# Last two output projections as one Strassen product inside the down projection, attention normalised by GpSimd, first two projections in groups of four

## The chip, the core and the metric

The kernel runs on one core of a Trainium2 chip, in one launch. The metric is device time in microseconds (us), the median of several runs. TensorE (PE in the profile) does the matrix products. VectorE (DVE) and ScalarE (ACT) do elementwise work and empty PSUM. GpSimd (POOL) takes some elementwise work. SyncE (SP) issues most of the DMA transfers, and POOL and ACT issue some. Each engine takes its own instructions strictly in their order and waits, with all that stands behind, for whatever its next instruction needs.

## The reference

One layer of a hybrid decoder, 2048 tokens of width 1024, all float32:

```python
    hn = rms_norm(h, mix_pre_g)
    proj = hn @ w_in
    q, k, v, u = ...
    attn_out = sliding_window_attention(q, k, v, attn_sinks, rel_bias)
    conv_out = conformer_conv(u, conv_dw, conv_dw_b, conv_ln_g, conv_ln_b, w_conv_pw)
    mixed = jnp.concatenate([attn_out, conv_out], axis=-1) @ w_out
    h = h + rms_norm(mixed, mix_post_g)
    hn = rms_norm(h, ffn_pre_g)
    ff = (jax.nn.silu(hn @ w_gate) * (hn @ w_up)) @ w_down
    h = h + rms_norm(ff, ffn_post_g)
```

Attention is banded (window 128, 8 query heads, 2 key heads, a learned sink per head); its softmax ends with `p = p / denom`. The convolution is depthwise with 31 taps on 512 channels, followed by LayerNorm, swish and a 512 x 512 product. `D_FF` is 2816.

## The kernel before

Four tiles of 512 tokens go through stages whose names carry the tile's number: A (in-projection), B (attention, in blocks of 128 tokens), T (the 31 convolution taps, `SCALAR_TENSOR_TENSOR` on DVE), C (the convolution's tail), W (output projection) with N (the two norms and the residual behind it), then for pairs of tiles H (the feed-forward's transposed operands), F (gate and up projections) and G (down projection). F0 and G0 serve tiles 0 and 1, F2 and G2 tiles 2 and 3. Stage J multiplies `w_conv_pw` into the lower half of `w_out` once (`w_join`), so that W's operand is the attention output above and the convolution's output below, kept transposed in DRAM as `mixT`.

Every float32 product is three TensorE passes: an operand is split into a high part (a copy by ACT) and a low part (a subtraction by DVE, sometimes POOL), and ah·wh, ah·wl and al·wh are accumulated in PSUM. A pass is a matmul of 128 x 128 by 128 x 512. F and G use one level of Strassen: seven products instead of eight, on sums of operand blocks.

W (`stage_w`) takes a tile's eight 128-row chunks of `mixT` two at a time (G=2): for each pair of chunks and each half of the output's columns it makes, for four blocks of 128 tokens, a PSUM group of six matmuls, and adds each group into an SBUF accumulator (the first by an ACT copy, the three others by DVE). W0 runs beside the end of A and W1 between A and F0; W2 and W3 stand in a lane beside G0, in the PSUM banks named `tr`, with accumulators in the SBUF buffers named `mid`.

N (`norm_w`) squares the accumulators on ACT, makes a reciprocal square root by some twelve tiny operations on POOL and DVE, scales on DVE, loads x and adds it, stores h, squares again, makes a second reciprocal root, scales on ACT (L841) and stores the result as `hn_scr` (L844). H (`stage_h_plain`) loads it back by columns (names `fc@H`, `at@H`), turns it on TensorE and makes the operands. Of F2 the products need B11 (from tile 2, four buffers `ql`) first and B21 (four buffers `mid`) second. `mid` is also where W3's accumulators are, so B21 of F2 can be made once tile 3's normalised rows have been stored.

F (`stage_p1`) writes each unit's products and their Strassen sums to DRAM (`mids<-fa@F`, the sums by DVE in F0 and by POOL in F2), and G (`stage_p2`) loads them back: the first two steps' operands through buffers `at`, the others through four buffers `fa`, the same that F's last sums use. G is 77 steps (7 products by 11 pairs of chunks), each 12 matmuls.

What sets the order: the main line of stages is a Python generator, and at each of its yields `run` pumps the lanes (`lb` attention, `lc` taps, `lw` projections, `lh` operands, `lt` sums, `ld` and `lf`), each at its own rate, so that the lanes' instructions are written between the main line's. A lane's stage may wait until another has come some way (`since`), and `until` writes a lane's rest at once. What is written first has priority, and a planner that works with its own durations then puts each engine's instructions in the order in which they are queued. `lc.rates` sets how early the taps of each tile are written: T3's are written slowly (RP 0.1) until F0 is over and at RC3 after.

The lines that the change touches: L518 (`vd`, the difference of neighbouring blocks of v) and L522 (the product by the reciprocal denominator, `p@B<-p@B,sm@B`) in `stage_b`; all of `stage_w`; the plan's last part, which adds W2, C3, W3 and B11.2 to `lw`, runs G0 and calls `lw.until("N3")`. Matmuls are L109 and most DVE operations L86, whoever calls them.

Of the kernel before, what the change touches and what calls it, by code (L numbers as in the profile page):

```python
# [25 lines left out]
P = 128  # L26
# [12 lines left out]
def layer_kernel(ctx, tc, x, xT, cols, rows, sinks, relb, onehot, w_in, w_pw, w_out, w_gate, w_up, w_down, out):  # L39
# [19 lines left out]
    def f4(tag, shape=(P, D)):  # L59
        return t_(tag, shape)  # L60
# [4 lines left out]
    def hl(tag):  # L65
        return t_(tag, (P, 2, T), F32R)
# [387 lines left out]
    def stage_b(t):  # L454
# [56 lines left out]
        def back(b):  # L511
# [3 lines left out]
            if not first:  # L515
                lab[0] = L
                vd = t_("vd", (P, P))
                vtt(vd, vtok[:, b], vtok[:, b + 1], ALU.subtract)  # L518
            for g in range(2):
                lab[0] = L  # L520
                hs = slice(4 * g, 4 * g + 4)
                vtt(pr[:, hs], pr[:, hs], rd[:, hs].unsqueeze(2).to_broadcast([P, 4, P]), ALU.mult)  # L522
                pg = f4("p", (P, 2, T))
                o = tr()
                for i in range(4):
                    nc.tensor.transpose(o[:, i * P : (i + 1) * P], pr[:, 4 * g + i], ident)
# [12 lines left out]
                yield 0.9  # L539
# [216 lines left out]
    def stage_w(w, spill, G, atag, htag, mtag, bank_of, norm=None):  # L756
        L = f"W{w}"
        lab[0] = L
        acc = [f4(atag) for _ in range(4)]

        def acts(gi, ms=None):
            aa = []
            for m in ms or load(gi):
                a = hl(htag)
                act(a[:, 0], m, AF.Copy)  # L765
                vtt(a[:, 1], m, a[:, 0].bitcast(F32), ALU.subtract)
                aa.append([a])
            return aa

        stage = spare_tile() if w == 1 else None  # L770

        def load(gi):
            ms = []
            for c in range(G * gi, G * gi + G):
                ms.append(stage[:, c % 2] if w == 1 else f2(mtag))
                nc.sync.dma_start(ms[-1], mixT[c, :, w * T : (w + 1) * T])
            return ms

        first = load(0)
        gb = load_gb(0) if w > 1 else None  # L780
        if w != 1:
            yield 5.0 if w == 0 else 8.0
            lab[0] = L
        nxt = acts(0, first)
        for gi in range(KC // G):
            aa = nxt
            for n in range(2):
                lab[0] = L
                if n == 0 and gi + 1 < KC // G:
                    if w < 2 and G * gi + G == 4:  # L790
                        ld.until(f"C{w}")
                        lab[0] = L
                    rows_next = load(gi + 1)
                if n == 1 and gi + 1 < KC // G:
                    nxt = acts(gi + 1, rows_next)
                src = w_out[2 * gi : 2 * gi + 2] if gi < 2 else w_join[2 * gi - 4 : 2 * gi - 2]
                ws = weight(src[:, :, n * T : (n + 1) * T].rearrange("c p t -> p c t"),
                            lo_out[n, 2 * gi : 2 * gi + 2], w > 0, on_pool=False)
                yield from block_half(acc, list(zip(aa, ws)), n, gi == 0, L, bank_of)
        tail = norm_w(w, spill, acc, mtag, gb)  # L800
        if norm:
            norm(tail)
        else:
            yield from tail

    def norm_w(w, spill, acc, mtag, gb):
# [377 lines left out]
    def stage_p2(ws, am, td, last=False):  # L1184
# [112 lines left out]
        for i in range(nn):  # L1297
            ty, pr = steps[i]
            load(i + 3)
# [91 lines left out]
    RC0, RC1, RC2, RC3, RW0, RW, RB, LC = 0.7, 1.1, 0.4, 0.9, 1.7, 1.25, 0.8, 100  # L1391
# [8 lines left out]
    RP = 0.1  # L1400
# [8 lines left out]
    JL, JS = 10, 2  # L1409
    lb = Lane(RB, 0)  # L1410
# [9 lines left out]
    lw.rates = {"W0": RW0, "C2": RW, "W2": RW, "C3": RW, "W3": RW}  # L1420
# [13 lines left out]
    lw.add("W0", stage_w(0, True, 2, "x", "hl", "fa", mm), lambda: "A3" in started and "J" in ld.done)  # L1434
# [53 lines left out]
    run(stage_w(1, True, 2, "mid", "hl", "at", mm, norm=lambda g: lh.add("N1", g)))  # L1488
# [8 lines left out]
    ws, ops = (2, 3), {}  # L1497
    lw.add("C2", stage_tail(2))
# [75 lines left out]
```

## Time and profile before

| | us |
|---|---|
| Median of three runs | 1947.46 |
| The three runs | 1943.13, 1947.46, 7967.86 |
| Profiled execution, its own time | 1948.75 |
| Profiled execution, span from first to last instruction | 1947.0 |
| PE busy | 1903.4 (98%) |
| DVE busy | 1488.2 (76%) |
| ACT busy | 971.4 (50%) |
| POOL busy | 231.7 (12%) |

The mean granted TensorE clock is 0.991. In the trace A and B fill the span up to about 440 us, W0 and W1 the time to about 550 us, F0 runs to 982 us, G0 to 1303 us, F2 to 1733 us, and G2 to the end. Each of these stages follows the one before on TensorE with no more than a few microseconds between. One of the three runs took four times as long as the others and says nothing of the kernel.

### The profile page before, as it was taken

How to read it: one execution, taken by the hardware profiler on the slowest of the kernel's cores; microseconds unless marked ns; L12 is line 12 of the kernel's file. 1: busy time of each engine (PE TensorE's matmuls, PEld its weight loads, DVE VectorE, ACT ScalarE, POOL GpSimd, SP SyncE). 2: the span in 40 equal slices, each digit the busy share in tenths (PEclk: the TensorE clock that was granted, in tenths of full speed). 3: DMA queues.
4: the chain of work that ended last, by engine and by line, in shares of the span. 5: the costliest groups of instructions: out<-in, count | busy, mean ns of one | idle time of the engine just before them, and what ended most of it. 6: DMA issues, size and time to landing. Idle time of an engine off the chain costs nothing.

```text
span 1947.0 us, 26776 instructions
## 1 busy us (share of the span) xinstructions
PE 1903.4 (98%) x8730; PEld 1538.9 (79%) x8730; DVE 1488.2 (76%) x2747; ACT 971.4 (50%) x1910; POOL 231.7 (12%) x327
## 2 busy tenths in 40 slices
PE   8999999999999999999999999999999999999997
PEld 7877776777778888878878878878888888888886
DVE  5999989897885999988569985778666665455557
ACT  5355444557667533433364556576533443345443
POOL 5100001221010000000000110010032332211000
PEclk9999999999899999999999999999999999999999
DMA  8896756579768776877487688689644443375664
GB/s 304 276 318 227 238 172 189 190 228 329 236 221 280 236 255 216 277 261 252 138 306 241 209 302 261 208 309 360 215 160 160 162 157 102 131 248 189 207 194 152
DMA packets 229181, 443.56 MB, mean 228 GB/s; under 512 B 22920, under 2 KB 48688, under 8 KB 229040
## 3 DMA queue, kind: packets, MB, share of 16 engines
q1 hardware_dynamic: 207408, 406.19, 63.1%
q10 hardware_dynamic: 19392, 28.32, 4.0%
q0 software_dynamic: 2240, 7.34, 1.0%
q8 instruction: 68, 1.11, 0.2%
q14 instruction: 73, 0.60, 0.1%
HBM read 320.64 MB, written 121.12 MB: 227 GB/s over the span
## 4 chain that ended last, share of the span: by engine, by line
PE 73%; DVE 12%; DMA 8%; issue 3%; ACT 2%; POOL 2%; SPq 0%; DVEq 0%; ACTq 0%; POOLq 0%
PE mm@F L109 36%; PE mm@G L109 16%; PE mm@A L109 8%; DVE fc@C L86 4%; PE tr@W L109 4%; PE mm@W L109 4%; PE tr@B L109 2%; DMA raw@A<-w_in 1%; PE ct@J L109 1%; DVE w@F L86 1%; DMA mixT<-fc@C 1%; DVE mid@W L86 1%; DMA at@W<-mixT 1%; DVE fa@F L86 1%; DMA hT<-gb@H 1%
## 5 line engine op out<-in xcount | busy, mean ns | idle before, releaser
L86 DVE SCALAR_TENSOR_TENSOR fc@C<-glu@C,colt,fc@C 128x512 f32<-128x512 f32 x480 | 354.7, 754 | 2.2
L109 PE MATMUL mm@F<-hl@H,w@F 128*128 128x512 f32 x1056 | 254.6, 390 | 0.8 <-ACT gb@F L1109 0.8
L109 PE MATMUL mm@G<-hl@G,hl@G 128*128 128x512 f32 x924 | 226.1, 395 | 6.1 <-DVE hl@G L86 2.2
L109 PEld LDWEIGHTS mm@F<-hl@H,w@F 128*128 128x128 f32 x1056 | 197.8, 188 | 42.3 <-ACT gb@F L1109 1.3
L109 PEld LDWEIGHTS mm@G<-hl@G,hl@G 128*128 128x128 f32 x924 | 172.3, 189 | 45.3 <-DVE hl@G L86 4.1
L109 PE MATMUL mm@A<-hl@A,w@A 128*128 128x512 f32 x840 | 204.4, 396 | 3.1 <-ACT hl@A L342 1.4
L856 ACT ACTIVATE w@F<-chl@F 128x512 fp32r<-128x512 f32 x220 | 135.5, 625 | 137.0 <-PE mm@F L109 131.6
L109 PE MATMUL mm@G<-w@G,hl@G 128*128 128x512 f32 x876 | 199.5, 389 | 0.0
L109 PEld LDWEIGHTS mm@G<-w@G,hl@G 128*128 128x128 f32 x876 | 164.4, 188 | 34.1
L109 PEld LDWEIGHTS mm@A<-hl@A,w@A 128*128 128x128 f32 x840 | 157.1, 189 | 41.3 <-issue 2.5
L86 DVE TENSOR_TENSOR w@F<-chl@F,w@F 128x512 fp32r<-128x512 f32 x198 | 144.9, 735 | 37.1 <-ACT w@F L856 36.7
L109 PE MATMUL mm@F<-ql@H,w@F 128*128 128x512 f32 x528 | 131.0, 391 | 2.5 <-ACT w@F L856 2.2
L109 PE MATMUL mm@F<-mid@H,w@F 128*128 128x512 f32 x528 | 131.0, 390 | 1.2 <-DVE mid@H L86 1.2
L109 PE MATMUL mm@F<-p@H,w@F 128*128 128x512 f32 x528 | 130.6, 393 | 0.0
L109 PE MATMUL mm@F<-x@H,w@F 128*128 128x512 f32 x528 | 128.4, 391 | 0.0
L109 PEld LDWEIGHTS mm@F<-ql@H,w@F 128*128 128x128 f32 x528 | 98.4, 188 | 23.7 <-ACT w@F L856 2.7
L109 PEld LDWEIGHTS mm@F<-p@H,w@F 128*128 128x128 f32 x528 | 100.2, 190 | 21.2 <-ACT at@F L1112 0.2
L109 PEld LDWEIGHTS mm@F<-mid@H,w@F 128*128 128x128 f32 x528 | 98.8, 188 | 22.5 <-DVE mid@H L86 1.6
L109 PEld LDWEIGHTS mm@F<-x@H,w@F 128*128 128x128 f32 x528 | 98.6, 188 | 21.9 <-issue 0.8
L156 ACT ACTIVATE w@A<-raw@A 128x512 fp32r<-128x512 f32 x110 | 67.5, 626 | 85.8 <-PE mm@A L109 51.4
L86 DVE TENSOR_TENSOR w@G<-raw@G,w@G 128x512 fp32r<-128x512 f32 x73 | 51.0, 699 | 68.3 <-ACT w@G L856 67.4
L109 PE MATMUL mm@W<-w@W,hl@W 128*128 128x512 f32 x384 | 99.5, 406 | 2.3 <-ACT hl@W L765 2.3
(307 smaller groups left out, 3188.4 us busy)
## 6 DMA issues: line engine op xcount, KB each, us to landing
mids<-fa@F SPq DMA_DIRECT2D x154, 256.0 KB, 2.6
raw@A<-w_in SPq DMA_DIRECT2D x55, 512.0 KB, 4.8
w@A<-lo_in SPq DMA_DIRECT2D x84, 256.0 KB, 3.7
fc@G<-mids SPq DMA_DIRECT2D x77, 256.0 KB, 3.4
fa@G<-mids SPq DMA_DIRECT2D x75, 256.0 KB, 5.0
w@W<-lo_out SPq DMA_DIRECT2D x48, 256.0 KB, 4.9
chl@F<-w_gate SPq DMA_DIRECT2D x22, 512.0 KB, 4.1
raw@F<-w_gate SPq DMA_DIRECT2D x22, 512.0 KB, 3.5
```

Of the source, the lines that this page charges most:

```text
L86: r = op(*args, **kw)
L109: r = nc.tensor.matmul(*args, **kw)
L156: act(w[:, 0], raw, AF.Copy)
L856: act(w[:, 0], x, AF.Copy)
```

## The change

Four parts.

1. **W2 and W3 become one Strassen product** (`stage_pair(3, 2)`): the two tiles' rows are the upper and lower blocks of the left operand, `w_out`'s two row halves and two column halves the blocks of the right one. Seven products of four chunks, four token blocks and three passes are 336 matmuls, instead of 2 x 192. The right operand's sums are made by POOL (`stage_wsums`: 16 subtractions and 16 DMAs that POOL issues, at the end of F0 and the start of G0), the left operand's by DVE (`stage_msums`: 16 sums, stored by SP, after the tails C2 and C3). The product stands in G0 at its step 58 of 77 (`BREAK`), through `between`: all of POOL's and DVE's sums must be written before. Tile 3's accumulators stay in `mid`, tile 2's are in `chl`. N2 is written from product 5 on (tile 2's accumulators are complete then), B11.2 and B21.2 behind it in the same lane, N3 after the product and after N2, and what is left of the lane behind G0 (`lw.until("B21.2")`).
2. **Attention's normalisation moves to POOL**: 32 products of 128 x 512 (L522) and 15 differences of 128 x 128 (L518), `vtt` before, `ptt` now.
3. **W0 and W1 take their chunks four at a time**: a PSUM group is twelve matmuls, and each accumulator half gets one ACT copy and one DVE addition instead of three. That is 16 additions of 128 x 512 fewer for each of the two.
4. **Rates**: RC2 0.4 to 0.45, RC3 0.9 to 1.0, RP 0.1 to 0.5, so that the last tile's taps are written mostly during F0 rather than during G0.

In all PE has 48 matmuls fewer, DVE 61 instructions fewer, ACT 8 more, POOL 79 more and SP 22 more.

```diff
-                vtt(pr[:, hs], pr[:, hs], rd[:, hs].unsqueeze(2).to_broadcast([P, 4, P]), ALU.mult)
+                ptt(pr[:, hs], pr[:, hs], rd[:, hs].unsqueeze(2).to_broadcast([P, 4, P]), ALU.mult)
...
-    def stage_w(w, spill, G, atag, htag, mtag, bank_of, norm=None):
+    def stage_w(w, acc_tag, norm=None):
...
+        for g in range(2):
             for n in range(2):
+                ws = weights(g, n)
+                units = list(zip(ops[g], ws))
+                if (g, n) != (0, 1):
+                    yield from block_half(acc, units, n, g == 0, L, mm)
+                    continue
+                ld.until(f"C{w}")
...
+    def stage_wsums():
+        for k in range(4):
+            t, u = (t_("chl", (P, 2, T)) for _ in range(2))
+            for to, src in ((t, w_out[k]), (u, w_join[k])):
+                tied(nc.sync.dma_start(to, src.rearrange("p (a b) -> p a b", a=2)))
+            yield 5
+            b11, b12, b21, b22 = t[:, 0], t[:, 1], u[:, 0], u[:, 1]
+            for to, o, p_, q_ in ((0, b11, b12, b11), (2, b12, b22, b12), (1, b22, b22, b11), (3, b21, b21, b22)):
+                ptt(o, p_, q_, ALU.subtract)
+                nc.gpsimd.dma_start(w_tsum[to, k], o)
+                yield 1
...
+    def stage_pair(top, low, accs):
+        acc_t, acc_l = accs
+        banks = [tr(), tr(), tr(), ct()]
...
+        def after(ty, b):
+            if ty in (0, 2):
+                act(c12, o, AF.Copy) if b % 2 else nc.vector.tensor_copy(c12, o)
+            elif ty in (1, 4):
+                nc.vector.tensor_copy(c11 if ty == 1 else c21, o)
+                act(o, c12, AF.Copy)
+            elif ty == 3:
+                vtt(c22, o, c12, ALU.subtract)
+            elif ty == 5:
+                vtt(c22, c22, o, ALU.add)
+            else:
+                act(c12, o, AF.Copy) if b % 2 else nc.vector.tensor_copy(c12, o)
...
+        for i, (ty, k) in enumerate(steps):
+            load(i + 3)
+            split(i + 2)
+            for b in range(4):
+                a, w = opsd[i]
+                for z, (x_, y_) in enumerate(((0, 0), (0, 1), (1, 0))):
+                    mat(banks[b], a[:, x_, ss(b)], w[:, y_], start=i == z == 0, stop=k == 3 and z == 2, skip_group_check=True)
+                if k == 3:
+                    after(ty, b)
+                yield 0.69
+            started.add(f"M{ty}.{k}")
...
         for i in range(nn):
             ty, pr = steps[i]
+            if between and i == BREAK:
+                yield from between()
...
-    RC0, RC1, RC2, RC3, RW0, RW, RB, LC = 0.7, 1.1, 0.4, 0.9, 1.7, 1.25, 0.8, 100
+    RC0, RC1, RC2, RC3, RW0, RW, RB, LC = 0.7, 1.1, 0.45, 1.0, 1.7, 1.25, 0.8, 100
-    RP = 0.1
+    RP = 0.5
+    BREAK = 58
...
-    lw.add("W2", stage_w(2, True, 2, "mid", "ql", "at", tr))
     lw.add("C3", stage_tail(3), lambda: since(lc, "T3", CS))
-    lw.add("W3", stage_w(3, True, 2, "mid", "ql", "at", tr, norm=lambda g: lw.add("N3", g)))
-    lw.add("B11.2", stage_h_plain(ws, ops, "B11", 0))
-    run(stage_p2((0, 1), mids[0], td))
-    lw.until("N3")
-    lh.add("B21.2", stage_h_plain(ws, ops, "B21", 4), lambda: since(lw, "N3", NS))
+    lw.add("MS", stage_msums(3, 2))
+
+    def between():
+        lt.until("WS")
+        lw.until("MS")
+        accs = [[f4(tag) for _ in range(4)] for tag in ("mid", "chl")]
+        pair = stage_pair(3, 2, accs)
+        while "M5.3" not in started:
+            yield next(pair)
+        lw.add("N2", norm_w(2, True, accs[1], "at"))
+        lw.add("B11.2", stage_h_plain(ws, ops, "B11", 0), lambda: since(lw, "N2", NS))
+        lw.add("B21.2", stage_h_plain(ws, ops, "B21", 4))
+        yield from pair
+        lh.add("N3", norm_w(3, True, accs[0], "at"), lambda: "N2" in lw.done)
+
+    run(stage_p2((0, 1), mids[0], td, between=between))
+    lw.until("B21.2")
```

Where the instructions stand differs at three places that matter for what follows. In the rows below a name is out<-in with the stage behind the @ and a buffer's number behind that, and `x3` is three of a kind in a row.

The first place is TensorE's queue where F0 ends and G0 begins. Before, these rows stand there (`mm@F` is F0's last product, `tr@W` is W2):

```order
L109 MATMUL mm@F0_1543_9246<-yt@H0_1076_6283,w@F0_1549_9284 128x512 x6
L109 MATMUL mm@F0_1543_9246<-mid@H0_1119_6481,w@F0_1549_9284 128x512 x3
L109 MATMUL mm@F0_1543_9246<-mid@H0_1144_6601,w@F0_1549_9284 128x512 x3
L109 MATMUL mm@G0_1550_9354<-hl@G0_1561_9376,hl@G0_1562_9379 128x512 x2
L109 MATMUL mm@G0_1551_9355<-hl@G0_1561_9376,hl@G0_1562_9379 128x512 x2
...
L109 MATMUL mm@G0_1552_9356<-hl@G0_1561_9376,hl@G0_1562_9379 128x512
...
L109 MATMUL mm@G0_1553_9357<-hl@G0_1559_9370,hl@G0_1560_9373 128x512 x3
L109 MATMUL mm@G0_1553_9357<-hl@G0_1561_9376,hl@G0_1562_9379 128x512 x3
L109 MATMUL tr@W2_1645_9773<-w@W2_1643_9767,ql@W2_1638_9755 128x512
L109 MATMUL tr@W2_1646_9785<-w@W2_1643_9767,ql@W2_1638_9755 128x512 x2
L109 MATMUL tr@W2_1645_9773<-w@W2_1643_9767,ql@W2_1638_9755 128x512
L109 MATMUL tr@W2_1652_9815<-w@W2_1643_9767,ql@W2_1638_9755 128x512 x2
```

Now the third step of G0 (its operands `hl@G0_1536` and `hl@G0_1537`, the latter from the first buffer `fa`) follows the first two directly:

```order
L109 MATMUL mm@F0_1515_9282<-yt@H0_1044_6230,w@F0_1521_9319 128x512 x6
L109 MATMUL mm@F0_1515_9282<-mid@H0_1087_6428,w@F0_1521_9319 128x512 x3
L109 MATMUL mm@F0_1515_9282<-mid@H0_1112_6548,w@F0_1521_9319 128x512 x3
L109 MATMUL mm@G0_1522_9387<-hl@G0_1533_9409,hl@G0_1534_9412 128x512 x2
...
L109 MATMUL mm@G0_1524_9389<-hl@G0_1533_9409,hl@G0_1534_9412 128x512
L109 MATMUL mm@G0_1525_9390<-hl@G0_1531_9403,hl@G0_1532_9406 128x512 x3
L109 MATMUL mm@G0_1525_9390<-hl@G0_1533_9409,hl@G0_1534_9412 128x512 x3
L109 MATMUL mm@G0_1522_9387<-hl@G0_1536_9417,hl@G0_1537_9420 128x512 x2
L109 MATMUL mm@G0_1523_9388<-hl@G0_1536_9417,hl@G0_1537_9420 128x512 x2
```

W2's matmuls, which stood between the second and the third step of G0, are gone from here; 18 matmuls of G0 are left between F0's last product and the third step.

The second place is DVE's queue at the same point, with F0's last Strassen sums (`fa@F<-fa@F,fa@F`). Before:

```order
L86 TENSOR_TENSOR fa@F0_1540_9228<-fa@F0_1540_9228,mm@F0_1543_9246 128x512
L86 TENSOR_TENSOR fa@F0_1536_9192<-fa@F0_1538_9210,fa@F0_1536_9192 128x512
L86 TENSOR_TENSOR fa@F0_1538_9210<-fa@F0_1532_9168,fa@F0_1538_9210 128x512
L86 TENSOR_TENSOR fa@F0_1532_9168<-fa@F0_1536_9192,fa@F0_1532_9168 128x512
L86 SCALAR_TENSOR_TENSOR fc@C3_1525_9113<-glu@C3_1524_9111,colt_73,fc@C3_1525_9113 128x512
L86 TENSOR_TENSOR ql@W2_1638_9755<-at@W2_1625_9685,ql@W2_1638_9755 128x512
...
L86 TENSOR_TENSOR fa@F0_1540_9228<-fa@F0_1540_9228,fa@F0_1532_9168 128x512
```

Now:

```order
L86 TENSOR_TENSOR fa@F0_1512_9264<-fa@F0_1512_9264,mm@F0_1515_9282 128x512
L86 SCALAR_TENSOR_TENSOR fc@C3_1367_8246<-glu@C3_1366_8244,colt_73,fc@C3_1367_8246 128x512 x3
L86 TENSOR_TENSOR fa@F0_1508_9229<-fa@F0_1510_9247,fa@F0_1508_9229 128x512
L86 SCALAR_TENSOR_TENSOR fc@C3_1367_8246<-glu@C3_1366_8244,colt_73,fc@C3_1367_8246 128x512
L86 TENSOR_TENSOR fa@F0_1510_9247<-fa@F0_1504_9205,fa@F0_1510_9247 128x512
L86 SCALAR_TENSOR_TENSOR fc@C3_1367_8246<-glu@C3_1366_8244,colt_73,fc@C3_1367_8246 128x512
L86 TENSOR_TENSOR fa@F0_1504_9205<-fa@F0_1508_9229,fa@F0_1504_9205 128x512
L86 SCALAR_TENSOR_TENSOR fc@C3_1367_8246<-glu@C3_1366_8244,colt_73,fc@C3_1367_8246 128x512 x5
L86 TENSOR_TENSOR fa@F0_1512_9264<-fa@F0_1512_9264,fa@F0_1504_9205 128x512
L86 SCALAR_TENSOR_TENSOR fc@C3_1367_8246<-glu@C3_1366_8244,colt_73,fc@C3_1367_8246 128x512 x5
```

Ten of T3's taps stand among the four sums now, and before there were one tap and two of W2's subtractions.

The third place is TensorE's queue where G0 ends and F2 begins (`tr@H` is a transpose for F2's operands; `ql@H` is B11, `mid@H` is B21). Before:

```order
L109 MATMUL mm@G0_1553_9357<-hl@G0_2115_12380,hl@G0_2116_12383 128x512 x3
L874 MATMUL tr@H2_2158_12603<-ident_68,at@H2_2157_12601 128x128 x4
L109 MATMUL mm@F2_2132_12486<-ql@H2_1999_11712,w@F2_2127_12471 128x512 x3
L109 MATMUL mm@F2_2132_12486<-ql@H2_2006_11739,w@F2_2127_12471 128x512 x3
L109 MATMUL mm@F2_2132_12486<-ql@H2_2010_11758,w@F2_2127_12471 128x512 x3
L109 MATMUL mm@F2_2132_12486<-ql@H2_2020_11799,w@F2_2127_12471 128x512 x3
...
L109 MATMUL mm@F2_2134_12502<-mid@H2_2139_12523,w@F2_2129_12477 128x512 x3
```

Now:

```order
L109 MATMUL mm@G0_1525_9390<-hl@G0_2046_12347,hl@G0_2047_12350 128x512 x3
L990 MATMUL tr@H2_1973_11981<-ident_68,fc@H2_1972_11979 128x128 x4
L109 MATMUL mm@F2_2063_12453<-ql@H2_1975_11989,w@F2_2058_12438 128x512 x3
L990 MATMUL tr@H2_1981_12015<-ident_68,at@H2_1980_12013 128x128 x4
L990 MATMUL tr@H2_1986_12039<-ident_68,fc@H2_1985_12037 128x128 x4
L109 MATMUL mm@F2_2063_12453<-ql@H2_1983_12023,w@F2_2058_12438 128x512 x3
L990 MATMUL tr@H2_1996_12086<-ident_68,at@H2_1995_12084 128x128 x4
...
L109 MATMUL mm@F2_2082_12572<-ql@H2_1998_12094,w@F2_2067_12480 128x512 x3
...
L109 MATMUL mm@F2_2065_12469<-mid@H2_2006_12138,w@F2_2060_12444 128x512
```

Seven of the eight groups of transposes for B11 and B21 stood inside G0 before, and all eight stand behind G0's last matmul now. Between that matmul and the first that reads B21 there are 36 matmuls of F2. From the pair's last matmul to G0's last there are 79 matmuls of G0.

More of the change, by code (lines that the diff above doesn't have):

```diff
@@ L800, in stage_w, with weights @@
-        tail = norm_w(w, spill, acc, mtag, gb)
+                ops[g].append([a])
+        def weights(g, n):
+            lab[0] = L
+            cs = slice(n * T, (n + 1) * T)
+            hs = []
+            for k in (0, 2):
+                src = (w_join if g else w_out)[k : k + 2, :, cs]
+                hs += weight(src.rearrange("c p t -> p c t"), lo_out[n, 4 * g + k : 4 * g + k + 2], w > 0, on_pool=False)
+            return hs
+        rows_ = load(0)
+        if not w:
+            yield 5.0
@@ L801, in stage_w @@
+        tail = norm_w(w, True, acc, mtag)
         if norm:
@@ L807, in norm_w @@
+    def norm_w(w, spill, acc, mtag, gb=None):
         L = f"W{w}"
@@ L1182, in finish, with stage_p2 @@
             lab[0] = L
-    def stage_p2(ws, am, td, last=False):
+    def stage_p2(ws, am, td, last=False, between=None):
         L = f"G{ws[0]}"
@@ L1487, in layer_kernel @@
         lh.add(n + ".0", stage_h_plain(ws, ops, n, off), lambda: since(lw, "W0", NH))
-    run(stage_w(1, True, 2, "mid", "hl", "at", mm, norm=lambda g: lh.add("N1", g)))
+    run(stage_w(1, "mid", norm=lambda g: lh.add("N1", g)))
     lc.hold = lambda: "S0" not in lh.done
```

129 lines of the change are left out of this document (92 added, 37 removed).

## The prediction

> **What bounds the kernel now.** I read the chain of work that ended last first, then the clock and TensorE's share by stretches, then the groups of the operations that change, then the tiles' rows at the two ends of G0. The chain by engine, the page's fourth part:
>
> ```profile
> PE 73%; DVE 12%; DMA 8%; issue 3%; ACT 2%; POOL 2%; SPq 0%; DVEq 0%; ACTq 0%; POOLq 0%
> ```
>
> TensorE carries the end. The busy time by stretches (start:end, length, then PE, PEld, DVE, ACT, POOL busy with counts, the granted clock, DMA's share, GB/s) shows how tightly: A and B with W0 and W1, then F0, G0, and a piece of F2 without any gap.
>
> ```profile
> 0.00:336.00 336.00, 323.12 (x1590) 251.37 (x1590) 297.62 (x639) 164.45 (x376) 51.85 (x78) 0.99 0.74 246
> 336.00:546.00 210.00, 204.35 (x1020) 157.65 (x1020) 179.37 (x432) 130.18 (x304) 32.09 (x73) 0.96 0.74 242
> 546.00:982.00 436.00, 432.24 (x1924) 353.23 (x1923) 353.51 (x580) 203.56 (x373) 12.65 (x28) 1.00 0.72 240
> 982.00:1303.00 321.00, 311.89 (x1401) 254.35 (x1400) 255.16 (x446) 184.41 (x327) 21.86 (x60) 0.99 0.79 262
> 1500.00:1750.00 250.00, 250.00 (x1105) 207.01 (x1103) 145.86 (x191) 97.02 (x172) 73.12 (x52) 1.00 0.46 158
> ```
>
> The last row gives the pace of a matmul when nothing disturbs: 250/1105 = 0.226 us. (A single row's 390 ns overlaps its neighbours.) F0 loses 3.8 us of 436 and G0 9.1 us of 321. So matmuls taken away are worth 0.226 us each, and every microsecond in which TensorE newly waits is added to the end. DVE is at 353.5/436 = 81% in F0: not the bound, but without much air.
>
> **Part 1a, fewer matmuls.** W2 and W3 cost 2 x 192 matmuls, the pair 336. 48 x 0.226 = **-10.9 us**. Copies, additions and splits of the pair go beside TensorE: DVE is at 255/321 = 79% in G0 and loses T3's taps there.
>
> **Part 1b, the cover where F0 ends.** G0's third step needs an operand that F0's last sums have stored and that is loaded back. Rows of F0's last product, of the DMA and split of `fa@G`, and of one of the last sums:
>
> ```profile
> L109 PE MATMUL mm@F<-mid@H,w@F x6: 389/389/389, 980.8 to 981.9; 128*128 128x512 f32 x6
> L1203 SPq DMA_DIRECT2D fa@G<-mids x5: 319/320/422, 992.6 to 1000.8; - x5
> L856 ACT ACTIVATE hl@G<-fa@G x2: 619/622/625, 998.9 to 1000.4; 128x512 fp32r<-128x512 f32 x2
> 987.39 2.14 DVE L86 TENSOR_TENSOR fa@F<-fa@F,fa@F 128x512 f32<-128x512 f32 x3 [4.13 <-DMA mids<-fa@F]
> 989.34 1.66 PE L109 MATMUL tr@W<-w@W,ql@W 128*128 128x512 f32 x6 [2.51 <-ACT ql@W L765]
> ```
>
> The last product ends at 981.9 + 0.4 = 982.3 and the high part of the operand is ready at 998.9 + 0.6 = 999.5: 17.2 us, set by two transfers in a row (sums wait 4.1 us for a store, the load is issued at 992.6), not by arithmetic. Before, TensorE does two steps of G0 there and then, from 989.3 on, W2. The order of the changed kernel has 18 matmuls of G0 in that place and nothing behind: 18 x 0.226 = 4.1. That leaves 17.2 - 4.1 = 13.1; 2.5 of it is idle before W2 already (last row), so 10.6 is new. The ten taps that now stand among the sums on DVE are partly in the gaps in which DVE waits for the store, and partly in the way; a tap lasts 0.744 us in F0 (row below), so they add 0 to 7.4. SP's loads for G0 stand behind the last store, as before. I take **+13**; ends +4 (the transfers pass in half the time, 17.2/2 - 4.1) and +20 (17.2 + 7.4 - 4.1).
>
> ```profile
> L86 DVE SCALAR_TENSOR_TENSOR fc@C<-glu@C,colt,fc@C 128x512 f32<-128x512 f32 x89 | 66.1, 744 | 0.1
> ```
>
> **Part 1c, the cover where G0 ends.** B21 of F2 lies in `mid`, and `mid` is free when tile 3's normalised rows are stored. How long the norm takes is shown by W3's rows: last addition, x added, second squares, scaling, store.
>
> ```profile
> L86 DVE TENSOR_TENSOR mid@W<-mid@W,tr@W x4: 686/686/687, 1239.6 to 1246.2; 128x512 f32<-128x512 f32 x4
> L86 DVE TENSOR_TENSOR mid@W<-wx@W,mid@W x1: 1218/1218/1218, 1258.1 to 1258.1; 128x1024 f32<-128x1024 f32 x1
> L834 ACT ACTIVATE junk<-mid@W x4: 1042/1052/1057, 1259.8 to 1285.3; 128x1024 bf16<-128x1024 f32 x4
> L841 ACT ACTIVATE mid@W<-mid@W,sm@W x4: 1135/1136/1137, 1295.2 to 1298.3; 128x1024 f32<-128x1024 f32 x4
> L844 ACTq DMA_DIRECT2D hn_scr<-mid@W x4: 326/326/327, 1296.3 to 1299.5; - x4
> DMA to landing us min/median/max: 2.7/3.7/6.2
> ```
>
> From the last addition's end (1246.9): 11.2 to the first addition of x, 28.2 to the end of the second squares (1286.3), 10.0 to the first store's issue (1296.3), 3.7 to its landing, and about 1.3 for the split of B21's first chunk: 54.4 us. Before, all of it lies under G0, which ends at 1303. Now it begins when the pair ends, with 79 matmuls of G0 left, 17.9 us, and 36 of F2 that need B11 alone, 8.2 us. Seven groups of four transposes come out of G0 into the same gap; as they are only moved, they neither cost nor cover more than their own time. So at least 54.4 - 17.9 - 8.2 = 28.3 is uncovered, even if N3 runs at once.
>
> It does not: N3 is written behind N2, and both load x through the same two `at` buffers. N2's last additions stand 43 matmuls (9.7 us) ahead of the pair's end in TensorE's queue, so N2 begins to add x at 11.2 - 9.7 = 1.5 us after it. W2's rows give a shorter duration for that phase:
>
> ```profile
> L86 DVE TENSOR_TENSOR mid@W<-wx@W,mid@W x1: 1215/1215/1215, 1127.6 to 1127.6; 128x1024 f32<-128x1024 f32 x1
> L834 ACT ACTIVATE junk<-mid@W x4: 1042/1057/1058, 1128.8 to 1151.1; 128x1024 bf16<-128x1024 f32 x4
> ```
>
> That is 24.6 us (1127.6 to 1152.2). Two phases in a row, then the tail of 10.0 + 3.7 + 1.3: 1.5 + 2 x 24.6 + 15.0 = 65.7 us, less the cover of 26.1 = 39.6; with W3's 28.2 it is 46.8. W0's norm, with x loaded through other buffers and little beside it, is the fast end:
>
> ```profile
> L86 DVE TENSOR_TENSOR x@W<-fa@W,x@W x6: 680/682/691, 456.4 to 466.7; 128x512 f32<-128x512 f32 x6
> L834 ACT ACTIVATE junk<-x@W x4: 1046/1052/1059, 458.3 to 468.4; 128x1024 bf16<-128x1024 f32 x4
> ```
>
> Its phase is 13.1 us (456.4 to 469.5): 1.5 + 2 x 13.1 + 15.0 - 26.1 = 16.6. I take **+38**, near W2's, since the two loads at a time are as in W2; ends +17 and +47. What is late next is F2's first B21 product, then nothing: F2's other operands are made from hT later.
>
> **The clock after a stall.** After a wait the granted clock is low for a while:
>
> ```profile
> 524.00:530.00 6.00, 4.95 (x13) 3.78 (x14) 4.31 (x16) 4.48 (x10) 0.64 (x1) 0.50 0.54 186
> 1125.00:1137.00 12.00, 9.53 (x33) 6.67 (x32) 10.04 (x17) 3.75 (x7) 0.00 (x0) 0.86 0.87 263
> ```
>
> At 0.50, 13 matmuls took 6.0 us instead of 2.9: 3.1 lost. At 0.86, 33 took 12.0 instead of 7.5: 4.5 lost, 2.5 of it idle. So 2 to 3 us for each of the two stalls: **+5**, ends +3 and +10. The Trainium skill ("TensorE: Matmul & The Clock Gate", Part 1: The HAM clock gate) says that an idle window of about 3.4 us drops the clock to half and that a busy window of the same length brings it back; by it, two stalls would cost some 2 x 1.7 = 3.4 us, an estimate, at the low end of mine.
>
> **Parts 2 to 4.** The rows for attention's product, for POOL at such work, for the start of POOL's reciprocal roots, and for DVE's additions in W:
>
> ```profile
> L86 DVE TENSOR_TENSOR p@B<-p@B,sm@B 128x512 f32<-128x512 f32 x32 | 21.1, 696 | 0.0
> L1131 POOL TENSOR_TENSOR fa@F<-fa@F,fa@F 128x512 f32<-128x512 f32 x33 | 46.0, 1395 | 58.1 <-DMA mids<-fa@F 30.8 <-DVE chl@F L86 14.6 <-issue 11.1
> L526 PE MATMUL tr@B<-ident,p@B 128*128 128x128 f32 x128 | 20.0, 281 | 0.0
> L182 POOL TENSOR_TENSOR sm@W<-sm@W x18: 199/201/4970, 448.1 to 1160.0; 128x4 f32<-128x4 f32 x18
> L86 DVE TENSOR_TENSOR x@W<-x@W,mm@W 128x512 f32<-128x512 f32 x24 | 15.9, 680 | 2.2 <-PE mm@W L109 2.1
> ```
>
> DVE is relieved of 21.1 us of products and of 32 x 0.68 = 21.8 us of W's additions, in stretches where it is busy 477 of 546 us. POOL gets 32 x 1.395 = 45 us; it has room (84 of 546 busy). The product takes 0.7 us longer, but TensorE waited 0.0 us for the transposes that read it, so I cost the move at nothing; what hides it are the projections that stand between. Ends: +22 (32 x 0.7, each on TensorE's path) and -18.6 (all of TensorE's idle time before 546: 546 - 527.5). Taps in F0: by the order some 70 more, at 0.744, add 52 us to 353.5, 93% of 436; F0's splits still come first in priority; 0, up to +8 (its idle time trebled). W2's and W3's own stall at 1125 to 1137 disappears with them: -3 of those 4.5. With -2 for A and W, "the rest" is **-5**.
>
> One rule speaks against part 2. A row to set beside it: two additions of the same form, on DVE in F2, the one while POOL works and the other not.
>
> ```profile
> L86 DVE TENSOR_TENSOR fa@F<-fa@F,gb@F 128x512 f32<-128x512 f32 x22 | 24.7, 1125 | 0.0
> L86 DVE TENSOR_TENSOR fa@F<-fa@F,at@F 128x512 f32<-128x512 f32 x22 | 15.0, 681 | 0.0
> ```
>
> The Trainium skill ("SBUF — State Buffer", Who interferes with whom) states that a DVE instruction with two SBUF inputs contends with a GpSimd instruction that reads SBUF, and that the loser waits for the whole instruction. The trace agrees so far: 1125 against 681 ns.
>
> **The sum**, against the profiled execution's own time: 1948.75 - 10.9 + 13 + 38 + 5 - 5 = 1988.9. That execution lies 1.3 above the median of 1947.46, so the median to expect is 1987.6, say **1988 us**.
>
> **The rivals.**
> - *The stalls are short.* If norms run at W0's pace (+17), F0's end costs +4 and the clock +3, the sum is 1947.5 - 10.9 + 4 + 17 + 3 - 5 = 1956: no change. For it: in the gap DVE and SP have little else to do. Against it: W2's and W3's x phase waits on transfers, which an idle DVE doesn't shorten.
> - *The cover suffices after all: faster.* It needs both ends of G0 without new waits: 1947.5 - 10.9 - 5 = 1932, and with only the pair's gain 1936.6. To be faster by over 2% (below 1908.5) it would need all of TensorE's idle time before 546 as well: 1932 - 16.6 = 1915, not even then. Against it: 54.4 us of chain over 26.1 us of cover.
> - *POOL makes attention slow.* Each product waits for DVE's long operations: 45 us of POOL at the ratio 1125/681 is 74 us, 29 more, and with the 22 of the longer products on TensorE's path up to +51; 1988 + 25 = 2013 if half of it shows. Point of decision: more than one of POOL's products behind a tap at a time. Against: 0.0 us of waiting by TensorE.
> - *The change removes less than it says.* The pair's four banks are emptied after each of its seven products by copies as long as W's additions (0.68 us): 28 x 0.68 = 19 us if TensorE waited each time, 2007. Against: twelve matmuls of G0 or of the other banks, 2.7 us, stand between a bank's last matmul and its next; the range holds it.
>
> **How the numbers follow.** Both stalls near my values: 0.50, and with POOL's rival (0.08) all of that is at or over the bound of about 2% that a measurement can tell from no change (1986.4); half a chance of the former lies close to the bound, so some of it counts as the same: slower 0.50. The short stalls (0.36) and part of the first case make the same: 0.47. Faster by over 2%: 0.03; faster at all, but within 2%: 0.10 of the 0.47. The likeliest case's own range is 1968 to 2008. For 8 in 10 the range must reach to the short stalls and not to the full cover: 1948 to 2014.
>
> **What would show it.** Right: in the changed kernel's trace a wait of TensorE of 10 to 15 us within 20 us after F0's last product, ended by `hl@G<-fa@G`; waits of 30 to 45 us in all between G0's last product and F2's first product with `mid@H`, ended by `ql@H` and `mid@H`; granted clock near 0.5 just behind; `tr@W` and `ct@W` matmuls 336 in number. Wrong: no gap over 5 us at either place; idle time of TensorE before 546 us grown by over 10 us; F0 longer than 445 us.

## The result and the profile after

The changed kernel takes 2019.49 us (median of 4 runs, 2017.63 to 2021.93) against 1947.95 us (four runs, one more than in the table above). The ratio, taken without the run of 7967.86 us, is 1.0377, 95% interval 1.0352 to 1.0401. It is slower, as forecast, but by 72 us instead of 40, and 5 us over the upper end of the range.

The profiled execution after has a span of 2018.8 us, 71.8 more than before. Cut at F0's last product, at G0's last product and at F2's first product with B21 (`mm@F<-mid@H`), the two executions differ so (starts of these matmuls, us):

| stretch | before | after | difference |
|---|---|---|---|
| start to F0's last product | 981.9 | 988.3 | +6.4 |
| to G0's last product | 319.4 | 333.9 | +14.5 |
| to F2's first product with B21 | 6.2 | 60.1 | +53.9 |
| to the last instruction | 639.5 | 636.5 | -3.0 |

F2's first products with B21, before and after, and the 79 matmuls of G0 that follow the pair in the changed kernel:

```profile
L109 PE MATMUL mm@F<-mid@H,w@F x24: 388/389/504, 1307.5 to 1316.9; 128*128 128x512 f32 x24
L109 PE MATMUL mm@F<-mid@H,w@F x45: 388/389/794, 1382.3 to 1399.8; 128*128 128x512 f32 x45
1304.48 18.07 PE L109 MATMUL mm@G<-hl@G,hl@G 128*128 128x512 f32 x79
```

Both ends of G0 carry it. TensorE's waits, grouped by what released them (total, times, longest), begin in the changed kernel with rows that were not among the long ones before:

```profile
PE mm@G L109 <- ACT hl@G L972: 21.4, 3, 17.0
PE tr@H L990 <- DMA fc@H<-hn_scr: 17.3, 1, 17.3
PE mm@F L109 <- ACT mid@H L1013: 8.9, 1, 8.9
PE tr@H L990 <- DMA at@H<-hn_scr: 8.1, 3, 3.7
```

17.0 us of the first row are G0's third step. The second and the fourth are tile 2's normalised rows on their way back, and the third is B21's first buffer `mid`, which tile 3's rows hold until they are stored. The stretches after (columns as in the prediction):

```profile
988.00:1075.00 87.00, 61.87 (x251) 48.17 (x250) 65.78 (x77) 25.81 (x47) 30.37 (x32) 0.84 0.95 354
988.00:1322.00 334.00, 302.55 (x1321) 245.79 (x1320) 222.60 (x342) 160.02 (x281) 41.08 (x68) 0.95 0.79 271
1322.00:1382.00 60.00, 19.73 (x71) 14.01 (x69) 37.27 (x95) 39.20 (x74) 8.69 (x36) 0.62 0.80 276
```

In the last 60 us TensorE ran 71 instructions at a granted clock of 0.62; at the prediction's pace they would need at most 16 us (about half of them are short transposes), and they were busy for 19.7. In the 87 us behind F0 it ran 251, which would need 57 and were busy for 61.9, and POOL was busy for 30 of the 87. The convolution taps on DVE between 980 and 1030 us, before and after:

```profile
L86 DVE SCALAR_TENSOR_TENSOR fc@C<-glu@C,colt,fc@C 128x512 f32<-128x512 f32 x14 | 10.4, 746 | 0.1
L86 DVE SCALAR_TENSOR_TENSOR fc@C<-glu@C,colt,fc@C 128x512 f32<-128x512 f32 x22 | 23.4, 1071 | 0.4
```

There are more of them, and on the mean each is 44% longer, beside POOL's weight sums. The load of G0's third step, issued at 992.6 before, is now issued at 1011.0, and TensorE takes up that step at 1015.1:

```profile
L1319 SPq DMA_DIRECT2D fa@G<-mids x5: 388/432/779, 1011.0 to 1020.7; - x5
L972 ACT ACTIVATE hl@G<-fa@G x2: 629/630/631, 1014.5 to 1021.7; 128x512 fp32r<-128x512 f32 x2
1015.14 4.64 PE L109 MATMUL mm@G<-hl@G,hl@G 128*128 128x512 f32 x12 [16.96 <-ACT hl@G L972]
```

At G0's other end, the rows of tile 2's norm (`chl@G`) and of tile 3's (`mid@G`): first squares (L928), x added (`at@W`), second squares (L950), store (L960).

```profile
L928 ACT ACTIVATE junk<-chl@G x4: 1042/1050/1058, 1289.3 to 1295.0; 128x1024 bf16<-128x1024 f32 x4
L86 DVE TENSOR_TENSOR chl@G<-at@W,chl@G x6: 685/692/694, 1307.5 to 1322.9; 128x512 f32<-128x512 f32 x6
L950 ACT ACTIVATE junk<-chl@G x4: 1057/1058/1058, 1307.7 to 1323.7; 128x1024 bf16<-128x1024 f32 x4
L928 ACT ACTIVATE junk<-mid@G x4: 1040/1055/1056, 1325.7 to 1333.3; 128x1024 bf16<-128x1024 f32 x4
L86 DVE TENSOR_TENSOR mid@G<-at@W,mid@G x6: 684/689/692, 1343.4 to 1367.1; 128x512 f32<-128x512 f32 x6
L960 ACTq DMA_DIRECT2D hn_scr<-mid@G x4: 326/326/327, 1377.6 to 1380.7; - x4
```

Tile 3's first squares begin at 1325.7, 1 us behind the end of tile 2's last, though the pair had ended at 1305. The two norms stand in a row; only tile 2's scaling and stores lie beside tile 3's squares.

### The profile page after: what moved, and what is told of

The parts are those of the page before. It is cut to its first block, busy times and chain, and to the rows that moved or that the text cites. A ratio compares the mean times of both kernels' runs of the same rounds, so it can differ in the third digit from the quotient of the medians.

```text
span 2018.8 us, 26851 instructions
## 1 busy us (share of the span) xinstructions
PE 1911.3 (95%) x8682; PEld 1541.1 (76%) x8682; DVE 1495.9 (74%) x2686; ACT 978.9 (48%) x1918; POOL 306.7 (15%) x406
## 5 line engine op out<-in xcount | busy, mean ns | idle before, releaser
L86 DVE SCALAR_TENSOR_TENSOR fc@C<-glu@C,colt,fc@C 128x512 f32<-128x512 f32 x480 | 374.1, 795 | 2.9
L109 PEld LDWEIGHTS mm@F<-x@H,w@F 128*128 128x128 f32 x528 | 98.3, 188 | 21.7 <-issue 1.6
L86 DVE TENSOR_TENSOR hl@G<-mb@G,hl@G 128x512 fp32r<-128x512 f32 x77 | 57.1, 742 | 50.4 <-ACT hl@G L972 50.3
```

The lines of the kernel that those rows point to most:

```text
L86: r = op(*args, **kw)
L109: r = nc.tensor.matmul(*args, **kw)
```

## The experiments

Times are medians; the kernel before, on the same chips, was at 1945 to 1948 us. Edits are against the changed kernel, or against the kernel before where that is said.

**1. Another buffer for G0's third step.**

```diff
-                rawa[i] = f2("fc" if last else "at" if i < 2 else "fa")
+                rawa[i] = f4("mid")[:, 0:T] if 2 <= i < 8 and not last else f2("fc" if last else "at" if i < 2 else "fa")
```

> The changed kernel, with the operands of G0's steps 3 to 8 loaded into the idle mid buffers instead of the fa buffers that F0's last sums still hold; all else as it is. Theory (TensorE waits after F0 because W2 no longer covers the way of the sums through DRAM, and the buffer, not the data, holds the third step): the waits of 3.9 + 17.6 + 3.0 + 2.2 us between 991 and 1048 us go to under 6 us in all. The pair cannot start earlier, since C3 and the sums set its start, so its end stands closer to G0's end (27 matmuls instead of 79, by the order) and the wait there grows by up to 52 x 0.226 = 12 us: net 2019 - 24 + 12 = about 2007 (2000 to 2012). Rival (the taps and POOL's sums beside G0's splits on DVE are what TensorE waits for): the waits stay above 15 us, no change.

Measured: 2026.55 us (2019.40 to 2028.78), no gain. The wait for the buffer was gone, but 11.1 us of wait for a split on DVE stood some 11 us further on, and TensorE stood still for 22 us between 986 and 1075 us, against 25 in the changed kernel. DVE was busy almost without a gap from 990 to 1025 us, its taps still slowed by POOL. So the rival held for this place. From G0's last product to the first with B21 it was 71 us instead of 60.

**2. The two norms side by side.**

```diff
-        lh.add("N3", norm_w(3, True, accs[0], "at"), lambda: "N2" in lw.done)
+        lh.add("N3", norm_w(3, True, accs[0], "at"))
```

> The changed kernel, with tile 3's norm written right behind the pair instead of after tile 2's norm. Theory (the two norms in a row are the long chain behind G0): tile 3's squares, root and scaling, 17.6 us between tile 2's last square and tile 3's first addition of x, move beside tile 2's additions of x; the wait between G0's last product and F2's first product with B21 falls from 59.8 us to 42 to 50; total 2003 to 2011. Rival (the chain is bound by the x loads through the two at buffers, as in my prediction's sum): under 4 us gained.

Measured: 2020.79 us, no gain. Tile 3's rows were stored 21.7 us sooner, but tile 2's 8.7 us later, and B21 no sooner: 77.8 us behind the pair's end, 78.0 without the edit. The rows of the two tiles' x additions and stores:

```profile
L950 ACT ACTIVATE junk<-chl@G x4: 1056/1057/1058, 1304.8 to 1332.6; 128x1024 bf16<-128x1024 f32 x4
L960 ACTq DMA_DIRECT2D hn_scr<-chl@G x4: 326/330/417, 1339.0 to 1342.1; - x4
L86 DVE TENSOR_TENSOR mid@G<-at@W,mid@G x6: 683/692/693, 1331.2 to 1347.8; 128x512 f32<-128x512 f32 x6
L960 ACTq DMA_DIRECT2D hn_scr<-mid@G x4: 326/326/327, 1355.9 to 1359.6; - x4
```

The result is the rival's, under 4 us; whether the two `at` buffers were the reason was not tested. Tile 2's last second square waited on ACT behind tile 3's work, and its loads by columns stood on SP behind tile 3's last store of h (1348.6 to 1349.2). What is late next is tile 2 itself: B11 and B21 are both made from its rows.

**3. The pair earlier.**

```diff
-            y = f2("fc")
+            y = f4("mid")[:, 0:T] if t > 1 else f2("fc")
...
-            th = f2("fc")
+            th = f4("mid")[:, 0:T] if t > 1 else f2("fc")
...
-    YL, YL2 = 12, 20
-    BREAK = 58
+    YL, YL2 = 12, 8
+    BREAK = 38
...
+    lw.rates = {"W0": RW0, "C2": 4.0, "C3": 4.0, "MS": 3.0, "N2": 1.2, "B11.2": 1.2}
```

> The changed kernel, with the last two tails' loads and results in the mid buffers instead of the fc buffers that the sums of w_down hold, the tails and sums written without pauses, and the pair allowed from step 38 of G0: by the order 264 matmuls of G0 stand behind the pair instead of 79. Theory (the wait behind G0 is the norms' chain less its cover): cover grows by 185 x 0.226 = 42 us, so the wait of 59.8 us falls to some 18 us and the total to 1975 to 1985; the wait at F0's end is untouched (over 20 us). Rival (an earlier pair collides with the taps, tails and POOL's sums on DVE and slows G0 itself): G0 grows by over 15 us, total over 1995.

Measured: 1992.40 us, 27 less. The pair ran from 1140 to 1265 us (1197 to 1304 before the edit), the wait behind G0 fell from 60.1 to 29.4 us, G0 grew by 3.7. The mechanism held, for two thirds of the size: from the pair's end to B21 it was 90 us instead of 78, now beside G0's own splits.

**4. The three together** (the buffer for steps 3 to 6 only).

> The three edits together; by the order 407 matmuls of G0 stand behind the pair. Theory: both waits go, and what is left is 48 matmuls fewer than before: 2019 - 24 - 52 = 1943, less the low clock behind the two waits, 5 to 9 us: 1933 to 1943, under the kernel before. Rival (GpSimd in attention, the taps in F0 or the larger groups cost by themselves): both waits gone and still over 1950.

Measured: 2010.12 us. The wait behind G0 was gone (6.6 us between the two matmuls of the table). But TensorE stood still for 38 of the 68 us behind F0, most of it in front of C2's transposes: 8.9 us for loads that had not landed and 16.3 us in one piece for C2's normalised rows, whose statistics stood on DVE behind eight taps that took 9.1 us beside POOL's sums:

```profile
988.00:1056.00 68.00, 29.84 (x108) 21.25 (x107) 45.74 (x62) 19.76 (x32) 17.95 (x28) 0.65 0.87 312
```

Neither forecast had that: a tail written early puts its transposes ahead of G0's matmuls in TensorE's queue.

**5. The buffer, and POOL's weight sums later.** The first edit, and:

```diff
-    lt.add("WS", stage_wsums())
+    lt.add("WS", stage_wsums(), lambda: "G0.14" in started)
```

> The first experiment's kernel (operands of G0's steps 3 to 8 in mid), with POOL's 16 weight sums started at step 14 of G0 instead of at F0's end. Theory now (with the buffer out of the way, what held G0's splits were DVE's taps and splits beside POOL's sums, 2.2 us each instead of 0.75; and behind both waits stands one chain from T3's taps over C2, C3, the sums, the pair and the two norms to B21, which no gap of TensorE makes longer or shorter): the waits of TensorE from 986 to 1075 us fall from 26 us to under 8 us, taps there last 0.75 us, and the total stays within 1 per cent of 2020, since the wait behind G0 grows by as much. Rival (the two waits are separate costs that add): total 2000 or less.

Measured: 2026.71 us, within 1 per cent as forecast. Taps beside F0's end last 743 ns again, TensorE stands still for 6 us between 986 and 1075 us instead of 25, and between 988 and 1250 us it works nearly at pace:

```profile
988.00:1250.00 262.00, 250.21 (x1102) 203.33 (x1101) 171.50 (x272) 125.27 (x219) 37.80 (x56) 0.98 0.83 285
1250.00:1310.00 60.00, 52.98 (x220) 42.62 (x218) 33.37 (x56) 30.33 (x57) 2.81 (x11) 0.91 0.59 189
1310.00:1391.00 81.00, 19.27 (x69) 13.63 (x68) 46.82 (x110) 43.36 (x82) 8.95 (x38) 0.59 0.75 257
```

G0's last product stands at 1250.4 us, but that is not 72 us gained: the 220 matmuls of the second row are the rest of the pair, which now ran behind G0. G0 and pair together ended at 1310, 12 us sooner than without the edits, and B21 came at 1391.5, 9 us later. So 20 us of waits less at F0's end did not make the kernel faster. Tails and pair start by their own clock, as the rows of the changed kernel and of this run show (C2's and C3's loads, their results' stores, the pair's matmuls in its fourth bank):

```profile
L614 SPq DMA_DIRECT2D fc@C<-y_scr x8: 319/382/721, 1044.1 to 1129.6; - x8
L644 SPq DMA_DIRECT2D mixT<-fc@C x8: 320/348/554, 1105.3 to 1191.6; - x8
L109 PE MATMUL ct@W<-w@W,ql@W x84: 389/389/389, 1198.6 to 1304.2; 128*128 128x512 f32 x84
```

```profile
L614 SPq DMA_DIRECT2D fc@C<-y_scr x8: 319/324/423, 1039.8 to 1121.7; - x8
L644 SPq DMA_DIRECT2D mixT<-fc@C x8: 319/320/547, 1098.3 to 1186.4; - x8
L109 PE MATMUL ct@W<-w@W,ql@W x84: 388/389/628, 1194.5 to 1309.8; 128*128 128x512 f32 x84
```

The pair starts only 4 us sooner. Its end is not settled by this run, because the second edit bears on it: POOL's late sums were stored until 1244 us, and the pair waited 6.4 us for them behind G0:

```profile
1257.14 1.65 PE L109 MATMUL tr@W<-w@W,ql@W 128*128 128x512 f32 x3 [6.38 <-ACT w@W L156]
```

**6. Attention back on DVE** (`vtt` instead of `ptt` in both places).

> The changed kernel with attention's 32 products and 15 differences back on DVE (part 2 of the change undone). Theory (TensorE does not wait for them either way): time of the changed kernel within 4 us, 2016 to 2024. Rival (POOL's slower products hold attention): 2009 or less.

Measured: 2008.60 us (2004.49 to 2013.69), 11 less. My theory fell, and the rival's time came true: F0's last product comes at 982.9 instead of 988.3, which is half of the gain. The rival's reason, slow products that hold attention, is not shown by it.

**7 to 9 and 12. The parts in the kernel before**: groups of four alone, tap rates alone, attention on POOL alone, and the three together, without the pair.

> The kernel before with W0 and W1 in groups of four alone (part 3). Theory (DVE's 32 additions fewer lie beside TensorE, and the weights are loaded in another rhythm): 1942 to 1952, no difference. Rival (W's longer groups wait for weights, as the 3.2 us at 511 us in the changed kernel says): 1953 to 1958.

> The kernel before with the tap rates of the change (RC2 0.45, RC3 1.0, RP 0.5) alone: T3's taps mostly in F0. Theory (DVE in F0 goes from 81 to some 90 per cent and its splits are late now and then, while G0 has its cover of W2 and W3): F0 ends 3 to 8 us later, G0 3 to 6 us shorter, total 1945 to 1955. Rival (the taps in F0 push the sums of w_down into G0, and with them C2, which is the chain's start, so that W2 with its convolution part is late): total over 1960.

> The kernel before with attention's products and differences on POOL alone (part 2). The sixth experiment gained 11 us by taking them off. Theory (in the changed kernel they cost 6 us before F0's end, where TensorE waits behind POOL's work in A and W, and they cost it in any kernel): 1951 to 1959. Rival (they cost only together with larger groups in W0 and W1, or with what follows F0): 1945 to 1950.

> The kernel before with parts 2, 3 and 4 together (attention on POOL, groups of four, tap rates), W2 and W3 as before. Theory (the parts' own prices add: 14 + 5 + 0 by the runs of each alone, and the pair with its chain is all the rest of the 72): 1958 to 1970. Rival (the taps in F0 and POOL beside DVE make each other worse, and the pair alone costs far less): 1985 or more.

| in the kernel before | us | ratio, 95% interval |
|---|---|---|
| part 3 | 1952.52 | 1.0020 (1.0003 to 1.0036) |
| part 4 | 1945.74 | 1.0006 (0.9988 to 1.0024) |
| part 2 | 1959.83 | 1.0071 (1.0053 to 1.0089) |
| parts 2 to 4 | 1958.71 | 1.0061 (1.0041 to 1.0082) |

The forecasts for part 4 and for the three together came true; part 3 lies between its theory and its rival, and part 2 lies 1 us over its range. Part 2 costs 0.7% here and 0.5% in the changed kernel (experiment 6); parts 3 and 4 cost little or nothing, and the three together no more than part 2. The pair with its chain is the rest: 2019.5 - 1958.7 = 61 us. With W2 and W3 unpaired, G0 nearly keeps its length under the new rates (321.7 us against 319.4 between the same matmuls as in the table): the early taps do little harm by themselves. In part 2's run the taps up to 600 us, 759 ns before, show a part of the price:

```profile
L86 DVE SCALAR_TENSOR_TENSOR fc@C<-glu@C,colt,fc@C 128x512 f32<-128x512 f32 x315 | 242.7, 790 | 2.3
L522 POOL TENSOR_TENSOR p@B<-p@B,sm@B 128x512 f32<-128x512 f32 x32 | 41.6, 1319 | 77.3 <-DVE sm@B L507 58.5 <-DVE sm@W L86 8.6 <-ACT w@W L156 3.8
```

That is 315 x 31 ns = 10 us more of DVE for taps alone, against the 25 us of work that it gave away. How this becomes 14 us of time is open: TensorE's waits there are spread over A, W and F0, none over 5 us, and which of them is whose was not settled.

**10 and 11. The chain made shorter**, with attention on DVE: the sums of `w_down` sooner (RT 0.6), tails and sums at rate 2, a pause of 12 instead of 20, BREAK 30, norms side by side; the tenth with RP 0.6, the eleventh with 0.5.

> The changed kernel with the chain from F0 to B21 made shorter: the sums of w_down written sooner (RT 0.6) so that they end in F0 and leave the fc buffers to C2, T3's taps sooner (RP 0.6), tails and sums at rate 2 with a pause of 12 instead of 20, the pair allowed from step 30, tile 3's norm right behind the pair, attention back on DVE; by the order 290 matmuls of G0 behind the pair. Theory (the chain of taps, sums, tails, pair and norms set the end of G0 and the start of F2; TensorE's work between F0's last product and the first with B21 is some 300 us against a chain of 394): the chain is 60 to 85 us shorter, total 1935 to 1960. Rival (what DVE, ACT and the DMA queue do there is the bound, not the chain's order): total over 1985.

> As the tenth, with T3's taps at the change's rate (RP 0.5). By the order the sums of w_down end 70 matmuls later and C2's loads stand 70 later, the rest is the same. Theory (C2's start is what the chain hangs on, not the last tap): within 10 us of the tenth, the later one by up to 15 us if the order's 70 matmuls are late in earnest. Rival (the taps are the bound): 15 us slower or more than the tenth, or faster, if taps in F0 hold up F0's splits.

Measured: 1978.80 and 1982.81 us. From F0's last product to B21 it is 360.2 and 357.6 us instead of 393.9: the chain was 34 to 36 us shorter, half of what I expected, and the tenth is 30 us faster than the sixth, which has the same attention. Which of its edits did it was not separated. The tenth's last tap was later behind F0 (39.4 against 35.2 us) and its time no longer, so the taps' rate matters little here. What is left is F0's end, with TensorE at 107 instructions in 51 us and DVE busy for 45 of them:

```profile
979.00:1030.00 51.00, 29.15 (x107) 22.08 (x106) 45.39 (x62) 13.72 (x23) 21.44 (x29) 0.70 0.82 287
```

**13 and 14. POOL's weight sums in F0** (`WS` added to the lane behind `TS`), without and with the buffer of the first experiment for steps 3 to 6.

> The tenth experiment's kernel, with POOL's 16 weight sums written in F0, behind the sums of w_down, instead of at F0's end. Theory (what is left at F0's end, 25 us of waits in the tenth, is partly DVE's last taps, splits and sums beside POOL's sums): the taps there last 0.75 us, the waits from 979 to 1030 fall below 15 us, the chain from F0's last product to B21 gets 10 us shorter; total 1963 to 1971. Rival (they are the wait for the way of F0's sums and C2's loads through DRAM): no change, 1975 to 1983.

> The thirteenth with G0's steps 3 to 6 in mid. Theory (with the chain short and POOL out of the way, the third step's buffer is at last a cost of its own): the waits from 979 to 1030 fall below 8 us; by the order 250 instead of 314 matmuls stand behind the pair, so up to 14 us may come back behind G0; total 1953 to 1968. Rival (the chain still sets the end): within 4 us of the thirteenth.

Measured: 1976.11 and 1989.56 us. In the thirteenth the signs came true, but the total lies in the rival's range: the taps at F0's end last 745 ns again (the tenth's and the thirteenth's rows from 980 to 1030 us below), TensorE stands still there for 11 us instead of 22 (8.8 of it in front of C2's transposes, whose loads had not landed, then 1.2 for the third step), and B21 comes 335.5 us behind F0's last product, 25 sooner than in the tenth. But F0 ends at 993.4 instead of 979.2: POOL's sums now stand beside F0's splits, where TensorE waits 3 to 5 us three times between 850 and 895 us. The gain at one place was mostly paid at the other. The fourteenth stands still for only 4 us behind F0, but F0 ends later still (1002.0), from there to B21 it is 343.8 us, and the whole is 13 us slower; its forecast failed, and why F0 ends later stays open. No kernel tried beats the one before.

```profile
L86 DVE SCALAR_TENSOR_TENSOR fc@C<-glu@C,colt,fc@C 128x512 f32<-128x512 f32 x26 | 26.1, 1030 | 0.2
L86 DVE SCALAR_TENSOR_TENSOR fc@C<-glu@C,colt,fc@C 128x512 f32<-128x512 f32 x29 | 20.9, 745 | 0.1
```

## Why the prediction was wrong

*Bounds and the 48 matmuls.* "Matmuls taken away are worth 0.226 us each, and every microsecond in which TensorE newly waits is added to the end" is the step that failed for G0. It held before. After the change a chain of dependent stages sets when B21 can come: the rest of the sums of `w_down`, whose buffers `fc` C2 needs (C2's first load stands at 1044.1, 55 us behind F0), C2, C3, the sums of `mixT`, the pair, tile 2's norm and tile 3's. From F0's last product to B21 it takes 394 us, while TensorE had only about 315 us of matmuls to put beside it (325.6 before, less 10.9). Experiment 5 takes 20 us of waits away in its first part and gains nothing, and the pair starts 4 us sooner; 3 and 10 shorten the chain and gain 27 and 30 us. So the waits were not terms that add, and the 10.9 us saved did not show. Added up stretch by stretch, the miss of 32 us is 9 at F0's end, 11 at G0's end with the clock, and 12 in the rest.

*F0's end, +13.* The place and the cause of the first wait, the operand from F0's sums through `fa`, were right. The size was 22 (25 us without a matmul up to 1075 us, 3 before): the load was issued 22 us behind F0's last product and not 10. DVE's taps and sums took up to 2.2 us each where POOL's weight sums ran beside them, which I had priced for attention and not here. Experiment 13, which differs from the tenth only in where these sums stand, shows that they were the reason: with the old buffers, the load is issued 11 us behind F0's last product where the tenth has it 25 us behind. How long the step itself would then wait is not shown, as C2's transposes hold TensorE ahead of it. As a term of the sum it was wrong as well, since by experiment 5 it lay beside the chain.

*G0's end, +38.* Place, releaser and cause were right, the size was 54. The cover was as counted (79 and 36 matmuls). TensorE stood still for 40 of these 60 us, inside the 30 to 45 that were given as a sign, but only because the transposes from G0 and the low clock filled the rest. The chain from the pair's end to B21's first split was 77 us and not 65.7: I had put tile 3's squares, root and scaling beside tile 2's additions of x, and they came after (1325.7 to 1342, 17 us); tile 2's additions were 6 us shorter than W2's. Experiment 2 puts them beside each other, and the chain from the pair's end stays at 78 us. The low clock, +5, is inside these two stretches: their instructions were busy for 81.6 us where pace would give at most 73, so it was too low by some 4 us.

*Parts 2 to 4, "the rest", -5.* The stretch to F0's last product became 6.4 us longer instead of 2 shorter. "TensorE waited 0.0 us for the transposes that read it, so I cost the move at nothing" is the step: I looked for TensorE waiting for POOL's product and not for what POOL's product does to DVE. (In the changed kernel they are 0.0 us still; part 2 costs its 11 to 14 us without such a wait.) The rule weighed there stood beside it: by the Trainium skill ("SBUF — State Buffer", Who interferes with whom), a DVE instruction with two SBUF inputs contends with GpSimd's reads and waits for the whole instruction. The runs agree (taps of 790 against 759 ns beside attention's products, 1071 against 746 beside the weight sums). The trace before had said it more loudly than I read it: the row of 1125 ns counts eleven additions in F0 too, 683 ns each, and in F2 alone the mean is 1566 ns against 679. Part 2 alone costs 14 us, less than a third of the rival's 51.

*Taps in F0* were costed at 0, and in experiment 8 the time does not show them.

*The rivals.* Short stalls and full cover fell. The one on POOL was right in sign and small. The one on the pair's four banks fell too: TensorE never waits while the pair runs.

```profile
1197.00:1304.00 107.00, 107.00 (x473) 88.59 (x472) 68.89 (x114) 55.97 (x100) 2.74 (x12) 1.00 0.74 251
```

## What to carry over

Before adding up waits, follow the longest chain of dependent stages through the stretch in which they lie and compare it with the work there of the engine that sets the time (here TensorE); where the chain is longer, a wait removed early in it only moves to its end. A saving that joins two independent stages into one (W2 early, W3 late, into a pair behind both) gives up slack, and the slack is to be counted like an instruction. Work given to GpSimd is to be priced by what it does to DVE's instructions with two SBUF inputs that run beside it, not only by its own duration.

## What the hardware showed that was not expected

A DVE tap of 0.75 us took up to 2.2 us, three times its length, while POOL started a subtraction of 1.3 us every 2.15 us (1006 to 1013 us in the changed kernel); so POOL's 16 weight sums, 21 us of POOL, were not free, and moving them from F0's end into F0 moved most of their cost with them. And a stretch of several waits kept the mean granted clock at 0.62 over 60 us (0.65 over 68 us in experiment 4); rows of single matmuls between the waits go up to 0.79 us, where an undisturbed one shows 0.39.
